# One transformer block on one core: ScalarE adds through PSUM in the last down-projection products, and the up projection's input sums are handed out 3, 3, 2, 2, 2, 0

## The chip, the cores and the metric

The kernel runs on one core of one Trainium2 chip. A core has a matrix engine (TensorE, PE in the profile; PEld is its weight load), a vector engine (VectorE, DVE), a scalar engine (ScalarE, ACT), a general engine (GpSimd, POOL) and a queue that starts transfers (SyncE, SP). Each engine works through its own list of instructions in order and waits on semaphores for the others. Matrix products land in PSUM, an accumulator memory of eight banks here; a tile `pall` of 128 x 4096 float32 covers all of them, 512 columns a bank. Everything else lies in SBUF or in the chip's main memory.

The metric is the device time of one execution, in microseconds (us).

## What is computed

One layer of a hybrid network for 1024 tokens of width 1024: a root-mean-square norm and an input projection, a sparse attention branch and a recurrent branch (RWKV7), gates, an output projection with a residual, and then a feed-forward part with a short convolution. The change touches only that last part (`w_up` goes from 1024 to 2 x 2816 columns, `w_down` from 2816 to 1024):

```python
def _conv_ffn(h, w_up, conv_w, w_down):
    u = h @ w_up
    u = lax.conv_general_dilated(u, conv_w[:, None, :], window_strides=(1,),
                                 padding=((CONV_WIDTH - 1, 0),),
                                 dimension_numbers=('NWC', 'WIO', 'NWC'),
                                 feature_group_count=u.shape[-1])
    a, b = jnp.split(u, 2, axis=-1)
    return (jax.nn.silu(a) * b) @ w_down
...
        x = x + _conv_ffn(_rms_norm(x, norm_ffn[l]), ffn_up[l], ffn_conv[l], ffn_down[l])
```

All values are float32. The kernel splits each operand into two float16 parts, high and low, and forms a product as three matrix products (high x high, high x low, low x high) that add up in one PSUM bank. Weights are scaled by `WS` = 256 before the split, so a finished bank holds 256 times the product and is multiplied by `WI` = 1/256 on its way out.

## The kernel before

Tokens are handled in two halves of 512 (h = 0 and h = 1), columns in blocks of 128. The program is written as one Python function that records instructions; a list scheduler with a simulated clock then decides the order of each engine's list. It takes the order of the program as a preference and keeps all data dependencies. `tc.issue_after(x)` adds one more rule: what is recorded inside comes behind `x` on `x`'s own engine.

**The up projection** has 22 pairs of column blocks (a for the SiLU, b for the product). For the first `NE` = 6 pairs the second half of the tokens is computed plainly, in the loop at line 1644: for each of six groups two series of 24 matmuls (`mm3`, called at line 1661, records them at L277), the convolution taps on ACT and DVE (`taps`, L1537 to L1542), and SiLU of the group before (`silu`, L1548 to L1550). The other 16 pairs (loop at line 1719) use a scheme with seven products of half size in place of eight (`prod`, L1675), which needs sums and differences of the inputs. These are T1 to T4, for four blocks k = 0 to 3. They are prepared by the generators `tprep(k)` (line 1559), each in three steps:

1. two subtractions on DVE (t3 and t1, L1569),
2. high parts of T3 and T1 on ACT (L1563), their low parts on DVE (L1564), and two further subtractions (t2 and t4),
3. high and low parts of T2 and T4 in the same way.

`TSTEPS` (line 68) says which generators take a step after each of the six plain groups; the steps come behind the group's last tap on ACT (`lasts[0]`). The first `prod` for pair 6 needs T1 and T2 of all four k. The low parts of the weights of the plain groups are made on DVE too (`split8`, L1609), and the weights run five groups ahead (`PFD`).

**The down projection** sums over 22 blocks of the hidden width, in the order `DSEQ` = "nnsnsnsn". An "n" (`plain`, line 1786) takes two blocks and, for each of 16 outputs (m = 0 to 7, h = 0 and 1), runs six matmuls into one bank (L1807) and adds the bank to the running sum `acc[m, h]` on DVE (L1809). An "s" (`combined`, line 1818) takes four blocks by the seven-product scheme: `product` (line 1871) runs 24 matmuls for four banks (L1878). Three of its seven products, o2, o3 and o4, belong to one quarter of the output alone and are added to `acc` on DVE (L1887, `key` is set); the other four (a, b, d, e) are added to side sums `sacc`. After the last "s" the side sums are folded into `acc` by `merge` (line 1923) on DVE (L1928, L1931, L1938, L1941) and POOL (L1934, L1935, L1942, L1943).

The small sums and merges wait in a list `todo`. `tick` (line 1756) takes one of them behind each DVE add. In the last "s" the order of the products is o1 (a), o2, o5 (e), o6 (b), o7 (d), o3, o4; `merge(2)`, twelve entries, is put into `todo` behind o7. Of these, j = 0 and j = 1 give POOL adds to `acc[4, 0]` and `acc[5, 0]` while o3 is recorded, ahead of o4, whose key is (4, 0). The last "n" (blocks 20 and 21) sends each finished `acc[m, h]` out (L1811).

Banks are taken from four tags of two banks each, so a bank returns after eight groups of six matmuls.

Of the kernel before, what the change touches and what calls it, by code (L numbers as in the profile page):

```python
# [11 lines left out]
AF = mybir.ActivationFunctionType  # L12
# [52 lines left out]
WK = (0, 200)  # L65
LV = 20
NEW = 4
TSTEPS = [(0, 0), (0, 1), (1, 1), (2, 2), (2, 3), (3, 3)]
PFD = 5
DSEQ = "nnsnsnsn"  # L70
GD = 6
# [9 lines left out]
WS = 256.0  # L81
WI = 1.0 / WS
# [84 lines left out]
def build(tc, D, dbg=None, upto=99):  # L167
    nc = tc.nc
    V, A, G, T = nc.vector, nc.scalar, nc.gpsimd, nc.tensor
    dbg = dbg or {}  # L170

    def load(t, src):
        return nc.sync.dma_start(t, src)

    with ExitStack() as ctx:
# [36 lines left out]
        def ps(tag):  # L212
            b = banks[tag]
            b.append(b.pop(0))
            return pall[:, 512 * b[-1]:512 * b[-1] + 512]
# [14 lines left out]
        H = [slice(0, 512), slice(512, 1024)]  # L230
# [1261 lines left out]
        with ExitStack() as st:  # L1492
# [18 lines left out]
            last = None  # L1511
            for k in range(8):
# [4 lines left out]
                last = V.tensor_sub(h2lo[1][k], hf, h2hi[1][k]).ins  # L1517
# [71 lines left out]
        def wraw(src, scale="A", behind=None):  # L1589
            rn_[0] += 1  # L1590
            x_ = rn_[0] // 2 % 2
            raw = (wp, fp)[x_].tile([128, 8, 128], F32, name="wraw", bufs=2)
            lastw[0] = load(raw, src).ins
            if scale == "A":
                with tc.issue_after(behind) if behind is not None else ExitStack():
                    A.activation(raw, raw, AF.Copy, scale=WS)
            elif scale == "G":
                G.tensor_scalar(raw, raw, WS, 0.0, op0=ALU.mult, op1=ALU.add)
            return raw
# [44 lines left out]
        for i in range(NE):  # L1644
            us = []
            if i == NE - 1:
                g_ = prep_up(NE)
                w = next(g_)
# [4 lines left out]
            for o in range(2):  # L1653
                n = 2 * i + o + PFD
# [4 lines left out]
                pj = pjs[o]  # L1659
# [7 lines left out]
            with tc.issue_after(lasts[0]):  # L1667
                for k in TSTEPS[i]:
                    next(tg[k])
# [12 lines left out]
        acc = {}  # L1682
# [36 lines left out]
        for i in range(NE, 22):  # L1719
# [26 lines left out]
            w = wn  # L1746
# [7 lines left out]
        todo = []  # L1754

        def tick(ins):
            if todo:
                with tc.issue_after(ins.ins):
                    todo.pop(0)()
# [6 lines left out]
        def pset(n):  # L1766
            r = []
            for _ in range(n):
                p = pring[0] % 12
                pring[0] += 1  # L1770
                tags = ["T%d%s%d" % ((2, 1, 4)[p // 4], c, p % 4) for c in "hl"]
                r.append([tf(t).tile([128, 512], F16, name="hh" + t[2], tag=t) for t in tags])
            return r

        def slot():
            n = wn_[0] % 4
            wn_[0] += 1
            if n % 2 == 0:
                return [wp.tile([128, 8, 128], F16, name=t, bufs=2) for t in ("whi", "wlo")]
            return [fp.tile([128, 8, 128], F16, name=t, bufs=2) for t in (("s12h", "s12l"), ("s34h", "s34l"))[n // 2]]  # L1780

        def cut(dst, src, e):
            A.activation(dst[0], src, AF.Copy)
            e.tensor_sub(dst[1], src, dst[0])  # L1784

        def plain(i0):
            hd_, wd_ = [], []
            for i in (i0, i0 + 1):
                raw = fp.tile([128, 2, 512], F32, name="thr", tag=("s12", "s34")[i % 2])
                hs = pset(2)  # L1790
                for h in range(2):
                    load(raw[:, h], th_d[h][i])
                    with tc.issue_after((seed, t_)[i0 // 2]) if i0 <= 2 else ExitStack():
                        cut(hs[h], raw[:, h], G)
                hd_.append(hs)
                w = slot()
                cut(w, wraw(D["f_dn"][i], behind=None if i0 else seed), V if i >= LV else G)
                wd_.append(w)
            yield
            for m in range(8):  # L1800
                for h in range(2):
                    pj = ps("PBAM"[(2 * m + h) % 4])
                    n = 0
                    for hs, (dh, dl) in zip(hd_, wd_):
                        hh, hl = hs[h]
                        for x, y in ((dh, hh), (dh, hl), (dl, hh)):
                            T.matmul(pj, x[:, m], y, start=(n == 0), stop=(n == 5))  # L1807
                            n += 1
                    tick(V.scalar_tensor_tensor(acc[m, h], pj, WI, acc[m, h], op0=ALU.mult, op1=ALU.add))  # L1809
                    if i0 == 20:  # L1810
                        nc.sync.dma_start(D["out"][m][:, H[h]], acc[m, h])  # L1811
# [6 lines left out]
        def combined(i0, first, last):  # L1818
# [52 lines left out]
            def product(ops_, n_, key, first=False):  # L1871
                w, hs = ops_
                for j in range(4):
                    pj = ps("PBAM"[j])
                    n = 0
                    for kp in range(2):
                        for x, y in ((0, 0), (0, 1), (1, 0)):
                            T.matmul(pj, w[x][:, 4 * kp + j], hs[kp][y], start=(n == 0), stop=(n == 5))  # L1878
                            n += 1
                    if key is None:  # L1880
                        d = sacc[n_, j]
                        if first:
                            A.activation(d, pj, AF.Copy, scale=WI)
                            continue
                    else:
                        d = acc[key[0] + j, key[1]]
                    tick(V.scalar_tensor_tensor(d, pj, WI, d, op0=ALU.mult, op1=ALU.add))  # L1887
# [12 lines left out]
            sums(2)  # L1900
            sums(3)
            product(o1, "a", None, first)
            o5 = sop(0, G)
            product(o2, None, (0, 0))
            flush()
            if last:
                merge(0)
            o6 = sop(1, V)
            product(o5, "e", None, first)
            o7 = sop(2, V)  # L1910
            product(o6, "b", None, first)
# [35 lines left out]
        seq, i0 = [], 0  # L1947
        for c in DSEQ:
            if c == "n":
                seq.append(plain(i0))  # L1950
                i0 += 2
            else:
                seq.append(combined(i0, "s" not in DSEQ[:len(seq)], "s" not in DSEQ[len(seq) + 1:]))
                i0 += 4
# [39 lines left out]
```

## Time and profile before

| | us |
|---|---|
| median of the runs | 1654.91 |
| the profiled execution | 1654.87 |
| its span, first to last instruction | 1653.1 |
| plain groups of the up projection, and the start of the seven-product part | about 1060 to 1148 |
| seven-product part of the up projection | about 1140 to 1430 |
| down projection | about 1430 to 1647 |
| its last "s" and last "n" | 1584.8 to 1647.3 |

The span is counted from the first to the last instruction; what lies around it is start and end of the program. Times in the text are microseconds from the start of the span. An engine is busy while an instruction of its own runs; a row of a group of instructions gives the line, the engine, the operation, what it writes and reads by the program's names, the shape, the count, the busy time in us, the mean duration in ns and the idle time in front of them with what ended it. In a timeline the brackets hold that idle time for one row. Successive instructions of one engine overlap a little, so the distance between starts is shorter than a duration: matmuls last 0.38 us and start every 0.216 us.

The middle of the down projection looks like this (columns: stretch, length, then the busy time of PE, PEld, DVE, ACT, POOL with instruction counts, the granted clock, DMA share, GB/s):

```profile
1507.00:1528.00 21.00, 21.00 (x99) 9.51 (x97) 18.89 (x26) 7.04 (x12) 9.55 (x7) 1.00 0.13 37
1528.00:1564.00 36.00, 36.00 (x168) 16.33 (x167) 29.92 (x40) 20.06 (x31) 27.72 (x21) 1.00 0.51 161
```

PE is busy there without a gap, in a plain pair (1507 to 1528) as in a combined block (1528 to 1564).

### The profile page before, as it was taken

How to read it: one execution, taken by the hardware profiler on the slowest of the kernel's cores; microseconds unless marked ns; L12 is line 12 of the kernel's file. 1: busy time of each engine (PE TensorE's matmuls, PEld its weight loads, DVE VectorE, ACT ScalarE, POOL GpSimd, SP SyncE). 2: the span in 40 equal slices, each digit the busy share in tenths (PEclk: the TensorE clock that was granted, in tenths of full speed). 3: DMA queues.
4: the chain of work that ended last, by engine and by line, in shares of the span. 5: the costliest groups of instructions: out<-in, count | busy, mean ns of one | idle time of the engine just before them, and what ended most of it. 6: DMA issues, size and time to landing. Idle time of an engine off the chain costs nothing. (4 is left out here: it accounts for less than half of the span.)

```text
span 1653.1 us, 30211 instructions
## 1 busy us (share of the span) xinstructions
PE 1617.4 (98%) x11856; PEld 851.6 (52%) x11856; DVE 1178.0 (71%) x1958; ACT 869.8 (53%) x1571; POOL 425.5 (26%) x344
## 2 busy tenths in 40 slices
PE   7999999999999999999999999999999999999997
PEld 3456555555555555666666444444444444444443
DVE  7545677778876548865558595598777777585898
ACT  5544675667657754556434453454554555645530
POOL 2101132021121220010001200214334333656756
PEclk9999999999999999999999999999999999999999
DMA  6352343232444456535555863453222223722402
GB/s 214 104 147 90 103 148 122 68 117 74 128 147 144 144 167 206 186 123 160 186 177 169 276 214 132 157 176 115 78 89 90 89 77 118 263 74 95 140 26 102
DMA packets 124687, 224.62 MB, mean 136 GB/s; under 512 B 16384, under 2 KB 45440, under 8 KB 124416
## 3 DMA queue, kind: packets, MB, share of 16 engines
q1 hardware_dynamic: 124544, 222.69, 40.6%
q8 instruction: 93, 1.52, 0.4%
q14 instruction: 50, 0.41, 0.1%
HBM read 153.86 MB, written 63.96 MB: 132 GB/s over the span
## 5 line engine op out<-in xcount | busy, mean ns | idle before, releaser
L277 PEld LDWEIGHTS <-whi 128*128 128x128 f16 x1808 | 173.1, 98 | 204.0 <-issue 9.0
L277 PE MATMUL pall<-hlo,whi 128*128 128x512 f16 x608 | 229.6, 379 | 2.1 <-DVE hlo L252 2.1
L277 PE MATMUL pall<-hhi,whi 128*128 128x512 f16 x608 | 229.2, 379 | 0.7 <-DVE zs L712 0.4
L277 PE MATMUL pall<-hhi,wlo 128*128 128x512 f16 x608 | 152.8, 379 | 0.0
L267 DVE SCALAR_TENSOR_TENSOR wlo<-wraw,whi 128x1024 f16<-128x1024 f32 (+1 forms) x98 | 109.7, 1119 | 56.6 <-PE pall L277 24.8
L265 ACT ACTIVATE whi<-wraw 128x1024 f16<-128x1024 f32 (+1 forms) x98 | 93.0, 950 | 107.7 <-PE pall L277 53.8
L672 DVE TENSOR_TENSOR pl<-pf,ph 128x512 f16<-128x512 f32 (+3 forms) x208 | 117.9, 577 | 38.9 <-ACT pf L671 38.0
L277 PEld LDWEIGHTS <-wlo 128*128 128x128 f16 x904 | 86.5, 98 | 98.0 <-issue 3.3
L670 ACT ACTIVATE ph<-pall 128x512 f16<-128x512 f32 (+3 forms) x208 | 99.8, 480 | 63.7 <-PE pall L665 33.2
L607 DVE TENSOR_REDUCE mp<-pall 128x1 f32<-128x512 f32 (+2 forms) x192 | 96.0, 516 | 36.1 <-PE pall L605 26.2
L671 ACT ACTIVATE pf<-pall 128x512 f32<-128x512 f32 (+3 forms) x208 | 100.5, 483 | 0.0
L1699 DVE SCALAR_TENSOR_TENSOR U<-pall,par,U 128x1023 f32<-128x1023 f32 x64 | 82.1, 1282 | 11.3 <-ACT U L1697 9.3
L1631 POOL TENSOR_TENSOR s<-wraw 128x512 f32<-128x512 f32 x16 | 28.0, 1748 | 191.2 <-DMA wraw<-f_up 183.6
L1402 POOL TENSOR_TENSOR b<-b,bonus 128x512 f32<-128x512 f32 x8 | 11.3, 1407 | 229.9 <-ACT b L1400 203.0
L694 POOL TENSOR_TENSOR onat<-onat,ot 128x256 f32<-128x256 f32 x32 | 29.5, 926 | 139.2 <-DVE ot L693 108.0
L675 PEld LDWEIGHTS <-ph 128*128 128x128 f16 x592 | 55.8, 96 | 16.1 <-ACT ph L670 3.0
L680 PEld LDWEIGHTS <-pl 128*128 128x128 f16 x592 | 55.6, 98 | 14.1 <-DVE pl L672 5.2
L1675 PEld LDWEIGHTS <-whi 128*128 128x128 f16 x384 | 37.6, 98 | 45.3
L1609 DVE SCALAR_TENSOR_TENSOR wlo<-wraw,whi 128x1024 f16<-128x1024 f32 (+1 forms) x35 | 47.6, 1360 | 17.2 <-PE pall L1675 12.9
L678 PEld LDWEIGHTS <-ph 128*128 128x128 f16 x592 | 55.9, 97 | 6.2 <-issue 1.3
L1809 DVE SCALAR_TENSOR_TENSOR acc<-pall,acc 128x512 f32<-128x512 f32 x80 | 51.7, 680 | 9.2 <-PE pall L1807 9.2
L1608 ACT ACTIVATE s12h<-s 128x1024 f16<-128x1024 f32 x16 | 16.9, 1056 | 67.3 <-POOL s L1632 66.0
(583 smaller groups left out, 4351.4 us busy)
## 6 DMA issues: line engine op xcount, KB each, us to landing
wraw<-f_up SPq DMA_DIRECT2D x56, 512.0 KB, 3.3
wraw<-w_t SPq DMA_DIRECT2D x46, 512.0 KB, 3.8
wraw<-f_dn SPq DMA_DIRECT2D x22, 512.0 KB, 3.4
sg_d<-zs SPq DMA_DIRECT2D x32, 256.0 KB, 2.4
wraw<-w_out SPq DMA_DIRECT2D x16, 512.0 KB, 3.8
th_d<-TH SPq DMA_DIRECT2D x32, 256.0 KB, 2.3
z_d<-zs SPq DMA_DIRECT2D x28, 256.0 KB, 2.8
x<-xT SPq DMA_DIRECT2D x24, 256.0 KB, 5.9
```

The lines of the kernel that those rows point to most:

```text
L265: A.activation(hi[:, :nk], raw, AF.Copy, scale=WS)
L267: V.scalar_tensor_tensor(lo[:, :nk], raw, WS, hi[:, :nk], op0=ALU.mult, op1=ALU.subtract)
L277: lastm[0] = T.matmul(ps, a[:, k], ks_(b, k), start=(n == 0), stop=(n == 3 * nk - 1)).ins
L607: V.reduce_max(mp[:, x, br, t:t + 1], pm[:, 0:(b1 - b0) * 128], axis=AX.X)
L670: A.activation(ph[0:nkey, rg], pa[0:nkey, rg], AF.Exp, scale=0.125)
L671: A.activation(pf[0:nkey, rg], pa[0:nkey, rg], AF.Exp, scale=0.125)
L672: V.tensor_sub(pl[0:nkey, rg], pf[0:nkey, rg], ph[0:nkey, rg])
L675: T.matmul(pov[:, t, :], ph[0:nkey, tk], vt[0:nkey, kb, g, 0:65], start=first, stop=False, skip_group_check=True)
L678: T.matmul(pov[:, t, 0:64], ph[0:nkey, tk], vt[0:nkey, kb, g, 65:129], start=False, stop=False, skip_group_check=True)
L680: T.matmul(pov[:, t, :], pl[0:nkey, tk], vt[0:nkey, kb, g, 0:65], start=False, stop=True, skip_group_check=True)
L1699: V.scalar_tensor_tensor(u[:, d:1024], c[:, 0:1024 - d], P("conv", 44 * (2 - d) + ci), u[:, d:1024], op0=ALU.mult, op1=ALU.add)
L1809: tick(V.scalar_tensor_tensor(acc[m, h], pj, WI, acc[m, h], op0=ALU.mult, op1=ALU.add))
```

## The change

Two edits.

The first sets `TSTEPS` anew: the twelve steps of the four generators are handed out 3, 3, 2, 2, 2, 0 to the six plain groups in place of 2 to each.

The second concerns additions to `acc`, in the last combined block (the three products with a `key`: o2, o3, o4, twelve banks) and in the last plain pair for h = 0 (eight banks). There ACT first writes 256 x `acc` into the bank (`seeded`), all six matmuls accumulate onto it (none starts the bank afresh), and ACT writes the bank times 1/256 back to `acc`. The DVE add is left out for these twenty banks. Entries of `todo` that hung on such an add are taken without an `issue_after` in `product`; in the last plain pair they are taken only at h = 1, so at every second bank.

```diff
-TSTEPS = [(0, 0), (0, 1), (1, 1), (2, 2), (2, 3), (3, 3)]
+TSTEPS = [(0, 0, 0), (1, 1, 1), (2, 2), (2, 3), (3, 3), ()]
...
+        def seeded(pj, src):
+            A.activation(pj, src, AF.Copy, scale=WS)
+
         def plain(i0):
...
                     n = 0
+                    sd = i0 == 20 and h == 0
+                    if sd:
+                        seeded(pj, acc[m, h])
                     for hs, (dh, dl) in zip(hd_, wd_):
                         hh, hl = hs[h]
                         for x, y in ((dh, hh), (dh, hl), (dl, hh)):
-                            T.matmul(pj, x[:, m], y, start=(n == 0), stop=(n == 5))
+                            T.matmul(pj, x[:, m], y, start=(n == 0 and not sd), stop=(n == 5), skip_group_check=sd)
                             n += 1
+                    if sd:
+                        A.activation(acc[m, h], pj, AF.Copy, scale=WI)
+                        nc.sync.dma_start(D["out"][m][:, H[h]], acc[m, h])
+                        continue
                     tick(V.scalar_tensor_tensor(acc[m, h], pj, WI, acc[m, h], op0=ALU.mult, op1=ALU.add))
...
                     pj = ps("PBAM"[j])
                     n = 0
+                    if key and last:
+                        seeded(pj, acc[key[0] + j, key[1]])
                     for kp in range(2):
                         for x, y in ((0, 0), (0, 1), (1, 0)):
-                            T.matmul(pj, w[x][:, 4 * kp + j], hs[kp][y], start=(n == 0), stop=(n == 5))
+                            T.matmul(pj, w[x][:, 4 * kp + j], hs[kp][y], start=(n == 0 and not (key and last)), stop=(n == 5),
+                                     skip_group_check=bool(key and last))
                             n += 1
+                    if key and last:
+                        A.activation(acc[key[0] + j, key[1]], pj, AF.Copy, scale=WI)
+                        if todo:
+                            todo.pop(0)()
+                        continue
                     if key is None:
```

## What I predicted, before the changed kernel had run

> **What bounds the kernel now.** I read the page's top first, then its chain, then a table of stretches around the two places that the diff touches, then each engine's timeline there.
>
> ```profile
> span 1653.1 us, 30211 instructions
> ...
> PE 1617.4 (98%) x11856; PEld 851.6 (52%) x11856; DVE 1178.0 (71%) x1958; ACT 869.8 (53%) x1571; POOL 425.5 (26%) x344
> ```
>
> TensorE (PE) is busy for 98% of the span, so a change that removes no matmul can win only PE's idle time, 1653.1 - 1617.4 = 35.7 us in the whole program, and what follows the last matmul. The stretches (columns: stretch, its length and the busy time of PE, PEld, DVE, ACT, POOL with counts, clock, DMA share, GB/s) say where some of it is.
>
> ```profile
> 1090.00:1110.00 20.00, 20.00 (x94) 9.10 (x93) 19.89 (x34) 12.29 (x19) 0.00 (x0) 1.00 0.54 183
> ...
> 1130.00:1150.00 20.00, 18.31 (x86) 8.23 (x85) 19.60 (x28) 7.96 (x13) 9.40 (x6) 1.00 0.45 158
> ...
> 1585.00:1600.00 15.00, 15.00 (x71) 6.82 (x70) 14.39 (x18) 8.13 (x13) 10.14 (x9) 1.00 0.10 35
> 1600.00:1610.00 10.00, 9.86 (x45) 4.21 (x44) 10.00 (x13) 3.77 (x6) 7.38 (x5) 1.00 0.16 52
> 1610.00:1620.00 10.00, 9.81 (x45) 4.39 (x45) 10.00 (x15) 1.06 (x1) 6.72 (x6) 1.00 0.01 2
> 1620.00:1630.00 10.00, 8.89 (x41) 3.80 (x39) 10.00 (x11) 0.00 (x0) 10.00 (x7) 1.00 0.00 0
> 1630.00:1640.00 10.00, 9.35 (x43) 3.89 (x41) 10.00 (x12) 0.00 (x0) 8.77 (x7) 1.00 0.21 80
> ```
>
> The reader is to see two things. At the end (from 1585) VectorE (DVE) has no free moment, PE loses time, and ScalarE (ACT) does almost nothing: 8.13 + 3.77 + 1.06 = 13.0 us in all. And between 1130 and 1150 PE loses 1.69 us in one piece. The PE timeline names both.
>
> ```profile
> 1147.96 0.38 PE L1675 MATMUL pall<-T1l,s12h 128*128 128x512 f16 x1 [1.69 <-DVE T1l L1564]
> ...
> 1584.80 0.38 PE L1878 MATMUL pall<-hhh,whi 128*128 128x512 f16 x1
> ...
> 1589.98 0.38 PE L1878 MATMUL pall<-hhh,s34h 128*128 128x512 f16 x1
> ...
> 1622.91 0.38 PE L1807 MATMUL pall<-hhh,s12h 128*128 128x512 f16 x1 [0.74 <-DVE acc L1887]
> ...
> 1645.78 0.38 PE L1807 MATMUL pall<-hhh,wlo 128*128 128x512 f16 x1
> ```
>
> Rows 1584.80 and 1589.98 are 24 matmuls apart (one product of four groups of six): 5.18 / 24 = 0.216 us a matmul. The end has seven such products (168 matmuls, L1878) and the last plain pair (96, L1807), 264 in all, so PE needs 264 x 0.2158 = 57.0 us. It took 1645.78 + 0.22 - 1584.80 = 61.2 us. So 4.2 us are gaps, each put down to a DVE operation that empties a bank late; TensorE has eight PSUM banks, one per group of six matmuls.
>
> **The first edit: input sums handed out 3, 3, 2, 2, 2, 0.** Nothing is added or removed. There are four generators of three steps. Before, group 5 (the last) still took the last two steps of k=3, and its T1l is the row that PE waits for at 1147.96. After, k=3 ends in group 4, one group of two matmul series earlier. That stall goes: -1.7 us. What is late next is nothing that I can find: the same timeline shows no other PE wait between 1150 and 1584, and whatever this stage feeds follows PE.
>
> What it costs: DVE does a part of this work earlier, in a stretch where it is busy 19.89 of 20.00 us. Step 1 is two subtractions, step 2 four, step 3 two.
>
> ```profile
> 1112.81 0.68 DVE L1564 TENSOR_TENSOR T1l<-t,T1h 128x512 f16<-128x512 f32 x1
> ...
> L1609 DVE SCALAR_TENSOR_TENSOR s34l<-wraw,s34h x4: 1207/1209/1217, 1077.7 to 1109.1; 128x1024 f16<-128x1024 f32 x4
> ...
> L277 PE MATMUL pall<-h2hi,s34l x32: 379/379/379, 1089.1 to 1137.3; 128*128 128x512 f16 x32
> ```
>
> After group 1 the hand-out is ahead by six subtractions of about 0.6 us, so DVE's other work is up to 3.6 us later. What PE waits for from that work is the low half of the next weights (L1609). The first s34l of that row is cut at 1077.7 and first multiplied at 1089.1, 11 us later; the last is cut at 1109.1, and its eight matmuls of 0.216 us end with the one at 1137.3, so they begin about 1135.8, 27 us later. 3.6 us fit into the smaller of the two. ACT's share (splits of T) runs where it is busy 12.29 of 20 us. I cost it at nothing; without that cover it would be at most 3.6 us. Value: -1.7, bounds -1.7 and +1.9.
>
> **The second edit: twenty adds leave DVE.** In the last combined block, the three products that go straight to `acc` (o2, o3, o4: 12 groups), and in the last plain pair the groups with h = 0 (8), lose their DVE multiply-add. Each gets two ACT passes: a seed of the bank with 256 x acc before the matmuls, and an eviction by 1/256 after them.
>
> ```profile
> 1640.09 7.25 DVE L1809 SCALAR_TENSOR_TENSOR acc<-pall,acc 128x512 f32<-128x512 f32 x12
> ...
> L1724 ACT ACTIVATE pall<-pall 128x512 f32<-128x512 f32 x16 | 9.4, 587 | 0.9 <-PE pall L1675 0.9
> ...
> L1739 ACT ACTIVATE u<-pall 128x512 f32<-128x512 f32 x16 | 9.3, 582 | 4.5 <-PE pall L1675 4.5
> ```
>
> Back to back the adds take 7.25 / 12 = 0.60 us each, so DVE loses 20 x 0.60 = 12.1 us. It is busy without a pause from 1586.3 to 1640.09 + 7.25 = 1647.34, 61 us; 49 us are left, less than the 57.0 us of PE. ACT's passes: no row shows a copy from SBUF into PSUM, so the seed is bounded by the two nearest forms, 0.58 (both ends in PSUM or out of it) and the 0.63 us of an SBUF copy below; I take 0.60 for each pass. 40 x 0.60 = 24 us on top of 13.0 is 37 of 61 us, so ACT has room. The Trainium skill says in "ScalarE: Activation LUTs", section "Rules for kernel authors", to put add and multiply on VectorE and not on ScalarE. This kernel's rows bear out half of it (1.2 us of ACT for 0.6 of DVE); it counts the engine's time, which here lies idle. By that rule alone the sum would carry 24 - 12 = +12 us, by the rows nothing.
>
> So the bank gaps, 4.2 us, can go. Bounds 0 and -4.2; I take -4.2, as 49 against 57 leaves DVE 8 us of room, and state separately what takes their place.
>
> **The new wait.** The old add read `acc` after the matmuls; the seed reads it before. Two seeds, of o4's groups 0 and 1, come behind adds of `merge` on POOL (L1934, then L1935), which the code hands out during o3. POOL waits there for DVE's partial sums.
>
> ```profile
> 1583.71 0.63 ACT L1783 ACTIVATE hhh<-thq 128x512 f16<-128x512 f32 x1 [5.36 <-PE pall L1807]
> ...
> 1614.66 1.27 POOL L1934 TENSOR_TENSOR sd<-sb,sd 128x512 f32<-128x512 f32 x1 [2.65 <-DVE sb L1931]
> ...
> 1621.13 2.25 POOL L1935 TENSOR_TENSOR acc<-acc,sd 128x512 f32<-128x512 f32 x1
> ...
> 1637.89 3.40 POOL L1943 TENSOR_TENSOR acc<-acc,sd 128x512 f32<-128x512 f32 x2
> ...
> L1935 POOL TENSOR_TENSOR acc<-acc,sd 128x512 f32<-128x512 f32 x4 | 6.9, 1735 | 1.2 <-DVE acc L1887 1.2
> ...
> L1934 POOL TENSOR_TENSOR sd<-sb,sd 128x512 f32<-128x512 f32 x4 | 6.0, 1490 | 3.3 <-DVE sb L1931 3.3
> ...
> L1887 DVE SCALAR_TENSOR_TENSOR acc<-pall,acc 128x512 f32<-128x512 f32 x12 | 7.9, 677 | 0.0
> ...
> L1931 DVE TENSOR_TENSOR sb<-sa,sb 128x512 f32<-128x512 f32 x4 | 4.6, 1141 | 0.0
> ```
>
> The order on POOL is sd0, sd1, acc of group 0, sd2, acc of group 1: the last ends at 1621.13 + 2.25 = 1623.4. DVE reaches the partial sums 4 x 0.60 = 2.4 us sooner (o2's adds are gone ahead of them), so I move that to 1621.0. A PE without gaps wants group 1 of o4 after 150 matmuls, at 1584.80 + 150 x 0.2158 = 1617.2, and its seed 0.7 us before. That is a wait of up to 4.5 us, if the written order stands. Against it: groups 2 and 3 of o4 need no add of POOL ahead of their seed and are 2 x 1.3 = 2.6 us of matmuls that the scheduler may place first. Behind the waiting seed on ACT stand o3's evictions and the next seeds, and PE waits for those too, but in the same stretch of time. I take the middle, +2.2, bounds 0 and +4.5. The other seeds read sums that are long done, or (rows 6 and 7) need POOL's adds by about 1636, and POOL's last of sixteen adds ended at 1641.3 with 3.3 + 1.2 us of waiting in it.
>
> A second page bears on POOL's speed: "SBUF — State Buffer" of the Trainium skill, section "SBUF: two separate sides", says that a DVE operation with two SBUF inputs and a POOL operation lock each other out. The last two rows fit that: 677 ns with one input in PSUM, 1141 ns for the add with both in SBUF while POOL works. The adds that leave DVE are of the first kind, so by that rule POOL gets no faster; without it five adds at the 1.27 of row 1614.66 would take 6.4 us and not the 8.7 to 1623.4, and the sum would be 2.2 us lower, with no wait left.
>
> **After the last matmul.** The results go out through SP, sixteen of 256 KB.
>
> ```profile
> 1646.00:1648.00 2.00, 0.16 (x1) 0.00 (x0) 1.34 (x3) 0.00 (x0) 0.00 (x0) 1.00 1.03 386
> 1648.00:1650.00 2.00, 0.00 (x0) 0.00 (x0) 0.00 (x0) 0.00 (x0) 0.00 (x0) 1.00 1.01 379
> ...
> DMA to landing us min/median/max: 2.0/3.3/4.2
> ```
>
> The twelve adds that DVE does at 0.60 us demand more than the 386 GB/s at which the DMA share stands at 1.0, so the last transfers queue. Paced by PE (one bank in 1.3 us, 202 GB/s) they would not. The last landing could then be 2.0 us after issue in place of 3.3: -1.3; the median row is the other end, 0. I take -1.0, since the pace lies at half the full rate.
>
> **Sum:** -1.7 - 4.2 + 2.2 - 1.0 = -4.7 us. The profiled execution took 1654.87 us (span 1653.1 and 1.8 around it), 0.04 under the median of the runs: 1654.87 - 4.7 = 1650.2 us. About 2% (33 us) is what a measurement of this kernel can tell from no change, and all the terms together are 7.2.
>
> **Rivals.**
> 1. No new wait, since the scheduler puts groups 2 and 3 of o4 first: 1654.87 - 1.7 - 4.2 - 1.0 = 1648.0. For it: 2.6 us of other matmuls, DVE with 8 us of room. Against it: POOL's order in the rows above.
> 2. The end is no shorter, because the seed wait eats the 4.2 us and the transfers still bunch; only the first edit pays: 1653.2. For it: 4.5 us by the written order.
> 3. Slower: POOL's add for group 1 of o4 ends no sooner than before, at 1623.4. Then the group starts at 1624.1, the 114 matmuls from there take 24.6 us, PE ends at 1648.7 and not 1646.0: +2.7 - 1.7 = 1655.9 with the transfers as they are. It decides from about 1622.4 on, where the loss equals the 1.7 of the first edit. For it: POOL waits for DVE's partial sums, whose order the scheduler may change. Against it: DVE is relieved before them.
> 4. ACT in the way: all twenty seeds are exposed, one behind another, 20 x 0.60 = 12 us: 1654.87 - 1.7 - 4.2 + 12 = 1661.0. Against it: 24 us of free ACT time and eight banks. This is what the ScalarE page's rule would make of it.
> 5. The first edit does not do what it says: another operation of DVE holds PE at 1146, or the crowded stretch takes it back. With the rest as forecast: 1651.9.
>
> **Chances.** Forecast 0.38, rival 1 0.25, rival 2 0.15, rival 3 0.10, rival 4 0.03, rival 5 0.09. The likeliest is 1650.2. Low end: every term at its best, 1654.87 - 1.7 - 4.2 - 1.3 = 1647.7, taken to 1647.2 for the rounding of rows. High end: between rivals 2 and 3, 1655.2, which leaves out rival 4 and most of rival 3. No case reaches 33 us either way: within 2% 0.985, faster 0.005, slower 0.01 for an order that the scheduler changes in a place that I do not see.
>
> **What would show it.** First edit: no row L1675 with a wait for T1l near 1147, and group 5 without T operations. Second: 20 fewer adds on L1809 and L1887, DVE with pauses after 1590, PE's waits for `acc` gone; in place of them a PE wait for an ACT write to `pall` near o4, or none (rival 1). End: less than 5.8 us (1653.1 - 1647.34) from the last add to the end of the span. Wrong would be a PE that still ends 61 us after the first matmul of the last combined block.

## The result, and the profile after

The changed kernel takes 1645.48 us (median of four runs, 1644.33 to 1646.61) against 1654.91 us for the kernel before on the same chip. That is the median of three runs; a fourth, at 1856.51 us, was a slow one and does not count. The ratio on record is 0.9946, with a 95% interval from 0.9934 to 0.9958 (the two medians alone give 0.9943). The forecast was 1650.2 us in a range from 1647.2 to 1655.2. The gain, 9.4 us, is twice the forecast's 4.7, and the time lies 1.7 us below the low end of the range. By the 2% bound the two kernels are the same, as forecast.

The top of the page, of the profiled execution of 1646.51 us:

```profile
span 1644.6 us, 30242 instructions
...
PE 1616.4 (98%) x11856; PEld 852.0 (52%) x11856; DVE 1164.0 (71%) x1938; ACT 891.4 (54%) x1611; POOL 424.2 (26%) x344
```

The counts are those of the diff: DVE has 20 instructions fewer, ACT 40 more, PE as many as before. The span is 8.5 us shorter. The stretches of the end, in the columns of the forecast's table (from 1584 to the end):

```profile
1584.00:1600.00 16.00, 16.00 (x75) 7.23 (x74) 15.27 (x20) 12.09 (x22) 12.08 (x8) 1.00 0.21 66
1600.00:1610.00 10.00, 10.00 (x48) 4.55 (x47) 9.29 (x14) 5.36 (x9) 6.58 (x6) 1.00 0.01 2
1610.00:1620.00 10.00, 10.00 (x48) 4.55 (x47) 10.00 (x8) 7.65 (x14) 10.00 (x7) 1.00 0.00 0
1620.00:1630.00 10.00, 10.00 (x48) 4.51 (x46) 7.75 (x8) 5.97 (x11) 10.00 (x7) 1.00 0.38 146
1630.00:1641.00 11.00, 10.97 (x51) 4.80 (x49) 3.88 (x5) 2.99 (x5) 3.60 (x3) 1.00 0.54 204
...
sum 60.60, PE 56.97 PEld 25.64 DVE 46.88 ACT 34.05 POOL 42.26; mean PE 9.49 PEld 4.27 DVE 7.81 ACT 5.68 POOL 7.04
```

Before, PE lost 0.14 to 1.11 us in each of these stretches from 1600 on; now it loses nothing. DVE is busy 46.88 us where 49 was estimated, ACT 34.05 us where 37 was. ACT's share, by groups of the same end (busy time, mean ns, idle time before), confirms the price of 0.60 us a pass that the kernel before had no row for:

```profile
L1787 ACT ACTIVATE pall<-acc 128x512 f32<-128x512 f32 x20 | 11.8, 597 | 7.9 <-DVE sd L1905 6.2 <-DVE acc L1819 1.2 <-DVE sb L1905 0.2
L1894 ACT ACTIVATE acc<-pall 128x512 f32<-128x512 f32 x12 | 6.8, 586 | 0.0
L1816 ACT ACTIVATE acc<-pall 128x512 f32<-128x512 f32 x8 | 4.8, 597 | 11.1 <-PE pall L1813 11.1
```

To cut the 8.5 us into pieces the reader needs a fixed point ahead of both edits. The first matmuls on L1508, which sum the squares for the feed-forward norm, are one. Their rows, first of the kernel before and then of the changed one (minimum, median and maximum ns, first and last start):

```profile
L1508 PE MATMUL pall<-sqs,ones x2: 592/592/592, 1048.5 to 1048.9; 128*128 128x512 f32 x2
```

```profile
L1508 PE MATMUL pall<-sqs,ones x2: 592/592/592, 1049.0 to 1049.4; 128*128 128x512 f32 x2
```

Everything ahead of this row is the same program, and yet it begins between 1047.8 and 1052.3 in the fourteen profiled executions of this study. That is run-to-run variation; "from the norm row" below means the span less the start of this row. Of three more rows of the changed kernel's PE timeline, the last two give the other cuts; the first is a small wait that the kernel before does not have, and e1 comes back to it:

```profile
1138.35 0.38 PE L1675 MATMUL pall<-h2h,whi 128*128 128x512 f16 x1 [0.21 <-DVE u L1542]
...
1583.82 0.38 PE L1890 MATMUL pall<-hhh,whi 128*128 128x512 f16 x1
...
1640.59 0.38 PE L1813 MATMUL pall<-hhh,wlo 128*128 128x512 f16 x1
```

| piece | before, us | after, us | difference | forecast |
|---|---|---|---|---|
| up to the norm row | 1048.5 | 1049.0 | +0.5 | 0 |
| norm row to the last combined block | 1584.8 - 1048.5 = 536.3 | 1583.8 - 1049.0 = 534.8 | -1.5 | -1.7 |
| its 264 last matmuls | 61.2 | 1640.59 + 0.22 - 1583.82 = 57.0 | -4.2 | -4.2 + 2.2 |
| behind the last matmul | 1653.1 - 1646.0 = 7.1 | 1644.6 - 1640.8 = 3.8 | -3.3 | -1.0 |

So two terms account for the miss: a new wait that did not come, and an end that shrank by 3.3 us in place of 1.0.

**Why no new wait came.** The seeds of o4's groups 0 and 1 do stand behind POOL's adds to `acc`. The two rows of the POOL timeline that answer to 1614.66 and 1621.13 of the kernel before:

```profile
1607.84 1.26 POOL L1952 TENSOR_TENSOR sd<-sb,sd 128x512 f32<-128x512 f32 x1 [0.63 <-DVE sb L1949]
...
1614.31 1.72 POOL L1953 TENSOR_TENSOR acc<-acc,sd 128x512 f32<-128x512 f32 x1
```

Counted from the first matmul of the block, POOL's add for group 1 now ends at 1614.31 + 1.72 - 1583.82 = 32.2 us, where it ended at 1623.38 - 1584.80 = 38.6 before. The forecast moved it by 2.4 us; it moved by 6.4. The DVE timeline says where the rest is from. Two of the products' input sums (the numbers in the names of `sq` shift by a few from kernel to kernel) in the kernel before, then in the changed one:

```profile
1596.02 1.04 DVE L1858 TENSOR_TENSOR sq__17159<-wraw,sq__17017 128x512 f32<-128x512 f32 x1
...
1602.86 0.68 DVE L1858 TENSOR_TENSOR sq__17177<-wraw,sq__17035 128x512 f32<-128x512 f32 x1
```

```profile
1575.49 0.68 DVE L1868 TENSOR_TENSOR sq__17161<-wraw,sq__17017 128x512 f32<-128x512 f32 x1
...
1581.02 0.68 DVE L1868 TENSOR_TENSOR sq__17181<-wraw,sq__17035 128x512 f32<-128x512 f32 x1
```

They have left the combined block for the plain pair ahead of it, and two sums of the same kind (`tq`, L1856) with them: about 3.5 us of DVE's work, done where DVE had room. DVE alone in four stretches, before and then after (columns: stretch, length, busy time and count, clock, DMA share, GB/s):

```profile
1575.00:1584.00 9.00, 7.36 (x12) 1.00 0.01 2
1584.00:1593.00 9.00, 7.79 (x10) 1.00 0.16 58
```

```profile
1575.00:1584.00 9.00, 9.00 (x13) 1.00 0.01 2
1584.00:1593.00 9.00, 8.97 (x12) 1.00 0.20 58
```

The program allows it because an entry of `todo` that is taken at o2, o3 or o4 no longer stands in an `issue_after` behind a DVE add. The scheduler may now put such an entry wherever its data allow, and at o2 the entries are input sums, whose data were there long before.

ACT, too, does not keep to the written order. The rows of its timeline that hold the seeds of o4:

```profile
1610.28 0.60 ACT L1787 ACTIVATE pall<-acc 128x512 f32<-128x512 f32 x1 [4.21 <-DVE sd L1905]
...
1613.86 0.60 ACT L1787 ACTIVATE pall<-acc 128x512 f32<-128x512 f32 x1 [2.00 <-DVE sd L1905]
...
1614.88 1.11 ACT L1787 ACTIVATE pall<-acc 128x512 f32<-128x512 f32 x2
...
1616.39 0.60 ACT L1787 ACTIVATE pall<-acc 128x512 f32<-128x512 f32 x1
```

The first two are groups 2 and 3, each right behind the DVE add (`sd`, the third and fourth of o7) that empties its bank. Group 0 is the first of the two seeds at 1614.88; the other belongs to the last pair. Group 1 is the one at 1616.39: it must stand behind POOL's add, which ended at 1616.03.

**Why the end shrank.** The SP queue of the kernel before: the last twelve issues as one row, then all sixteen by duration (minimum, median and maximum ns, first and last start). Behind it, the changed kernel's last issue and its times from issue to landing (2.0/3.3/4.2 before):

```profile
1640.79 8.51 SPq L1811 DMA_DIRECT2D out<-acc  x12
...
L1811 SPq DMA_DIRECT2D out<-acc x16: 332/390/1805, 1634.5 to 1648.8; - x16
```

```profile
1641.79 0.33 SPq L1821 DMA_DIRECT2D out<-acc  x1
...
DMA to landing us min/median/max: 2.0/2.0/4.3
```

Most of the 8.51 us is the pace of DVE's adds, one in 0.60 us, which the issues follow; an issue itself takes 0.39 us in the median, and one took 1.80. The last one came at 1648.8, 1.5 us after the last add ended (1647.34), and the last add ended 1.3 us after the last matmul. Now DVE's last add follows its matmul at once, and SP issues at once:

```profile
1641.07 0.69 DVE L1819 SCALAR_TENSOR_TENSOR acc<-pall,acc 128x512 f32<-128x512 f32 x1 [1.90 <-PE pall L1813]
```

The 3.3 us are thus three: the last add 0.4 us nearer to the last matmul (1641.76 - 1640.8 = 1.0 against 1.3), its transfer issued 1.4 us sooner behind it, and 1.5 us less from there to the end (1644.6 - 1641.8 = 2.8 against 4.3). They are stretches of one chain and not three causes: e12 takes most of the second away, and the third grows by nearly as much.

### The profile page after: what moved, and what is told of

It is laid out like the page before. It is cut to its first block, busy times and chain, and to the rows that moved or that the text cites. A ratio compares the mean times of both kernels' runs of the same rounds, so it can differ in the third digit from the quotient of the medians.

```text
span 1644.6 us, 30242 instructions
## 1 busy us (share of the span) xinstructions
PE 1616.4 (98%) x11856; PEld 852.0 (52%) x11856; DVE 1164.0 (71%) x1938; ACT 891.4 (54%) x1611; POOL 424.2 (26%) x344
## 4 chain that ended last, share of the span: by engine, by line
PE 60%; DVE 6%; ACT 2%; issue 1%; DMA 1%; POOL 0%; DVEq 0%; ACTq 0%
PE pall L277 18%; PE pall L1675 18%; PE pall L1890 7%; PE pall L1813 6%; PE pall L297 3%; PE pall L1227 1%; PE pall L1171 1%; DVE u L1540 1%; PE pall L1318 1%; DVE t L1569 1%; PE pall L1373 1%; PE pall L1378 1%; PE pall L1275 1%; PE pall L1268 1%; PE pall L1334 1%
## 5 line engine op out<-in xcount | busy, mean ns | idle before, releaser
L1675 PEld LDWEIGHTS <-whi 128*128 128x128 f16 x384 | 37.5, 98 | 45.8 <-issue 0.7
L1609 DVE SCALAR_TENSOR_TENSOR wlo<-wraw,whi 128x1024 f16<-128x1024 f32 (+1 forms) x35 | 48.5, 1385 | 17.9 <-PE pall L1675 12.5
L1819 DVE SCALAR_TENSOR_TENSOR acc<-pall,acc 128x512 f32<-128x512 f32 x72 | 47.1, 681 | 16.4 <-PE pall L1813 15.3
```

Of the source, the lines that this page charges most:

```text
L1675: T.matmul(bank, w[wi][:, o_ + k], xs_[k][xi], start=start and n == 0, stop=n == 11, skip_group_check=True)
```

## The experiments

The expectations give the theories letters, and not always the same. In e1 and e2, A says that the two edits are independent. In e4 and e8, A says that the adds must leave DVE; C, there and in e6, that the freed order does most of it, by letting DVE's sums go sooner. In e3, e10 and e11 it is A that stands for the freed sums; its rivals are B, the adds alone, and F, the freed merges at o3 and o4. In e5, A is both edits to the products together. D: the end is long where results bunch in the transfers; E: a landing takes a fixed 2.0 to 3.3 us and transfers run side by side; G: it is SP that issues too slowly. Kernels named e1 to e4, e5 to e8 and e9 to e12 each ran on one chip, with runs of the kernel before in between (medians 1656.16, 1656.17 and 1654.28 us); a ratio is against those. The columns in us are from one profile of each, cut as above: "gaps" is what the 264 last matmuls took over 57.0, "end" is what follows the last of them. In the six kernels without gaps these matmuls take 57.0 us, alike within 0.02. (Where an expectation gives the end of the change as 3.6 us, it is counted from the end of the last matmul's row, 1640.59 + 0.38.)

| kernel | from the norm row | gaps | end | median | ratio, 95% interval |
|---|---|---|---|---|---|
| before | 604.6 | 4.2 | 7.1 | | |
| the change | 595.6 | 0 | 3.8 | 1645.48 | 0.9946 (0.9934 to 0.9958) |
| e1, steps only | 602.9 | 4.3 | 6.4 | 1653.47 | 0.9988 (0.9976 to 0.9999) |
| e2, adds only | 596.6 | 0 | 3.8 | 1647.81 | 0.9959 (0.9944 to 0.9973) |
| e3, adds on ACT, all entries tied | 597.0 | 1.8 | 3.8 | 1648.63 | 0.9960 (0.9945 to 0.9975) |
| e4, adds on DVE, entries free | 597.8 | 0.9 | 5.2 | 1647.57 | 0.9954 (0.9939 to 0.9969) |
| e5, ACT in the products only | 595.2 | 0 | 3.9 | 1646.73 | 0.9945 (0.9922 to 0.9967) |
| e6, ACT in the last pair only | 599.4 | 4.1 | 4.0 | 1650.43 | 0.9969 (0.9949 to 0.9989) |
| e7, last results recorded together | 595.2 | 0 | 3.8 | 1645.56 | 0.9933 (0.9912 to 0.9954) |
| e8, e6 with entries free | 596.3 | 1.1 | 3.8 | 1646.94 | 0.9947 (0.9927 to 0.9966) |
| e9, last results held together | 600.6 | 0 | 9.3 | 1651.62 | 0.9979 (0.9965 to 0.9994) |
| e10, only the sums tied | 597.3 | 2.1 | 3.8 | 1649.54 | 0.9972 (0.9960 to 0.9983) |
| e11, only the merges tied | 595.3 | 0 | 3.9 | 1646.81 | 0.9954 (0.9934 to 0.9974) |
| e12, before, with two queues | 604.6 | 4.4 | 6.9 | 1653.73 | 0.9997 (0.9986 to 1.0009) |

### e1 and e2: one edit at a time

e1 is the kernel before with the new hand-out:

```diff
-TSTEPS = [(0, 0), (0, 1), (1, 1), (2, 2), (2, 3), (3, 3)]
+TSTEPS = [(0, 0, 0), (1, 1, 1), (2, 2), (2, 3), (3, 3), ()]
```

> Only the input sums are handed out 3, 3, 2, 2, 2, 0; the down projection is as before. Theory A (the two edits are independent; the changed kernel's stretch from the norm at 1049 to the last combined block is 1.35 us shorter): 1653.4 us, PE's wait for T1l gone, a wait of 0.2 us at the first L1675, and the end as before (4.2 us of gaps, 7.1 us from the last matmul to the end of the span). Rival: the earlier hand-out costs what it saves, 1654.5 to 1655.

e2 is the changed kernel with the old hand-out, the same two lines the other way round.

> Only the adds move to ACT; the input sums are handed out as before. Theory A: PE waits 1.7 us for T1l as before, then no gap in the last 264 matmuls (-4.2) and 3.6 us from the last matmul to the end in place of 7.1 (-3.5): 1647.2 us, ratio 0.9953. Rival (the edits help each other, the end is short only if PE comes early): 1649 or more.

The waits of PE in e1, and then in e2 (who waits on whom: total us, times, longest):

```profile
PE pall L1675 <- DVE u L1542: 0.4, 1, 0.4
```

```profile
PE pall L1675 <- DVE T1l L1564: 1.2, 1, 1.2
```

In e1 the wait for T1l is gone, and a smaller one, for the convolution's taps, has come in. It is not a stall that the old one had hidden: the matmul that waits is the first on L1675, 10 us ahead of the old stall. The last operation of these taps and this matmul in the kernel before, then the taps in the changed kernel (its matmul is the row at 1138.35 above):

```profile
1136.35 0.14 DVE L1542 TENSOR_TENSOR u<-u,edge 128x2 f32<-128x2 f32 x1
...
1137.47 0.38 PE L1675 MATMUL pall<-h2h,whi 128*128 128x512 f16 x1
```

```profile
1138.12 0.14 DVE L1542 TENSOR_TENSOR u<-u,edge 128x2 f32<-128x2 f32 x1
```

Counted from the norm row, the taps end at 1136.49 - 1048.5 = 88.0 us before and at 1138.26 - 1049.0 = 89.3 in the change, and PE is ready for them at 1137.47 - 1048.5 = 89.0. So DVE, with input sums handed to it earlier, reaches the taps 1.3 us later, and that uses up the 1.0 us that PE had to spare. (In e5 they are 0.6 us later, at 1138.27 - 1049.7 = 88.6, and PE does not wait.) A wait shows in e1, the change and e4 (0.2 to 0.4 us) and in none of the other eight kernels with the new steps.

From the norm row to the last combined block the kernels with the old steps take 536.3 (before), 535.8 (e2) and 536.3 us (e12). With the new ones it is 535.2 (e1), 534.8 (the change) and 534.7 us (e4) where the taps wait, and 534.4 us in each of the other eight. Against the mean of the first three, 536.1, the first edit brings 1.7 us without that wait and 0.9 to 1.4 with it. The gaps and the end belong to the second edit: e1 keeps its 4.3 us of gaps, e2 has none.

### e3 and e4: the passes or the order

e3 is the changed kernel with the entries at o2, o3 and o4 held again behind a DVE add, the last one before them:

```diff
         def tick(ins):
+            lv[0] = ins
...
                         if todo:
-                            todo.pop(0)()
+                            with tc.issue_after(lv[0].ins):
+                                todo.pop(0)()
                         continue
```

> The changed kernel, but the entries of todo taken in o2, o3 and o4 are held behind DVE's last add of the product before them, near to where the old tick put them. Theory A (untying let the scheduler draw four sums, 3.5 us of DVE, from o2 into the plain pair before, and that is why POOL's adds came 7.4 us sooner and not the 2.4 of the adds alone): the two L1868 rows come back behind 1590, the first merged sd starts about 3 us later, PE waits 0.5 to 2 us near o4: 1646 to 1647.5. Theory B (the adds alone are enough): the same rows move, but PE has no gap and the time is that of the changed kernel, 1645.5 within 0.6.

e4 leaves all twenty adds on DVE and only frees the entries:

```diff
                         d = acc[key[0] + j, key[1]]
+                    if key and last:
+                        V.scalar_tensor_tensor(d, pj, WI, d, op0=ALU.mult, op1=ALU.add)
+                        if todo:
+                            todo.pop(0)()
+                        continue
```

> The new hand-out of input sums, all adds on DVE as before, but the entries of todo taken in o2, o3 and o4 are not held behind DVE's adds. Theory C (the order alone is most of the gain): DVE has 3.5 us less to do behind 1585, 57.5 against PE's 57.0, gaps of at most 1.5 us, and 1649 to 1650.5. Theory A (it takes the adds off DVE): gaps of 3 to 4 us remain and the end still takes 6 to 7 us: 1652 to 1653.4.

| gaps / end, us | entries tied | entries free |
|---|---|---|
| adds on DVE | 4.3 / 6.4 (e1) | 0.9 / 5.2 (e4) |
| adds on ACT | 1.8 / 3.8 (e3) | 0 / 3.8 (the change) |

Freeing the entries, with not one add moved, takes out 3.4 us of gaps; moving the adds with the entries tied takes out 2.5. The passes and the order both have a part, and the parts overlap. (In e3 all entries of a product hang on one add ahead of it, a looser tie than in e1, so 2.5 is rather too much for the adds. Its median is above the 1647.5 us expected at most, e4's below the 1649 that theory C gave.) At the end the passes are worth more (2.6 us against 1.2), as DVE must have caught up with PE by the last bank. The timed ratios of e3 and e4 cannot be told apart, which agrees with 597.0 against 597.8 us. Nor do the intervals of e4 and of the change lie apart: that the passes add something to the freed order (595.6 against 597.8 us) rests on the profiles. What is left in e4 is of the old kind: the matmuls on L1807 wait twice, 0.4 us in all, for a bank that DVE's adds to `acc` (L1888) empty late.

### e5, e6 and e8: which of the passes

e5 moves only the twelve adds of the products:

```diff
-                    sd = i0 == 20 and h == 0
+                    sd = False
```

> The changed kernel, but the last plain pair adds on DVE as before; only o2, o3 and o4 go through ACT, untied. Theory A (the product's adds and their untying end the gaps, the plain pair's adds only shorten the end): no gap or one of under 0.5 us in the last 264 matmuls, 4 to 5.5 us after the last matmul, 58 + 4.5 = 61 to 62.5 us from the last combined block's first matmul to the end (60.6 in the changed kernel, 68.3 before). Rival (the plain pair carries it): gaps of 1 us or more.

e6 moves only the eight of the last pair; `product` is as before, entries tied:

```diff
-                    if key and last:
+                    if False:
                         seeded(pj, acc[key[0] + j, key[1]])
...
-                    if key and last:
+                    if False:
                         A.activation(acc[key[0] + j, key[1]], pj, AF.Copy, scale=WI)
```

> The changed kernel, but o2, o3 and o4 add on DVE and their entries of todo hang on these adds, as before; only the last plain pair goes through ACT for h = 0. Theory C (most of the gaps come from the tied order in the product): gaps of 2 to 3.5 us up to the first plain groups, then none; the end at 3.6 to 4.5 us, since half of the results no longer wait for DVE: 63 to 65 us from the block's first matmul to the end. Rival (eight adds less are enough): gaps under 1 us.

e8 is e6 with the entries freed as in e4.

> The changed kernel, but o2, o3 and o4 add on DVE, with their entries of todo not held behind these adds; the last plain pair goes through ACT for h = 0. Theory C (untying is what the product needs, ACT there is not): no gap or under 0.7 us, 3.6 to 4 us after the last matmul, 60.6 to 61.5 us from the block's first matmul to the end. Theory A (the twelve adds must leave DVE too): gaps of 0.9 us or more, as with all adds on DVE, 61.5 us or more.

The eight passes of the last pair bring nothing once the other twelve are there: e5 takes 595.2 us from the norm row, the change 595.6, and its end, 3.9 us, is below the 4 to 5.5 that was expected. Alone, in e6, they turn DVE's lateness into a wait of another name. The longest PE wait of e6's timeline, and the only one of e8's:

```profile
1623.40 0.38 PE L1813 MATMUL pall<-hhh,s12h 128*128 128x512 f16 x1 [1.39 <-ACT pall L1787]
```

```profile
1627.98 0.38 PE L1813 MATMUL pall<-hhh,s12h 128*128 128x512 f16 x1 [0.86 <-ACT pall L1787]
```

A seed cannot go into a bank before DVE has emptied it, nor before the sum that it carries is complete. Where DVE is late, the seed is, and the matmul waits for ACT in place of DVE. e6's 4.1 us of gaps are nearly those of e1 (4.3) and above the 2 to 3.5 that theory C gave; of the 3.5 us that it gains over e1, 2.4 lie in the end. e8's 1.1 us of gaps speak for theory A: with the entries free, the last microsecond of gaps goes only when the twelve adds of the products leave DVE too.

### e10 and e11: sums or merges

Both are e3 with a condition. e10 holds only the entries at o2, the sums; e11 holds those at o3 and o4, the merges (`!=` in place of `==`):

```diff
+                            with tc.issue_after(lv[0].ins) if key == (0, 0) else ExitStack():
+                                todo.pop(0)()
```

> The changed kernel, with only the four sums that are taken in o2 held behind DVE's last add before it; the merge entries in o3 and o4 stay free. Theory A (the sums, 3.5 us of DVE drawn into the plain pair before, are what untying brings): most of the 1.8 us of gaps with everything held come back, 1 to 2 us, by PE waits for an ACT seed. Rival F (the merge order is what matters): no gap.

> The changed kernel, with only the merge entries taken in o3 and o4 held behind DVE's last add before them; the sums in o2 stay free. Theory A: no gap or under 0.5 us. Rival F: 1 to 2 us of PE waits for an ACT seed.

e11 equals the change (595.3 and 595.6 us, no gap), e10 has all of e3's loss and a little more. F falls: it is the input sums at o2. The profile of e10, DVE, POOL, ACT and PE in turn, shows the chain that the forecast had looked for, with another holder:

```profile
1596.13 0.68 DVE L1871 TENSOR_TENSOR sq__17161<-wraw,sq__17017 128x512 f32<-128x512 f32 x1
...
1619.45 0.68 DVE L1909 SCALAR_TENSOR_TENSOR sd<-pall,sd 128x512 f32<-128x512 f32 x1
```

```profile
1620.16 0.60 ACT L1790 ACTIVATE pall<-acc 128x512 f32<-128x512 f32 x1 [2.00 <-DVE sd L1909]
...
1620.61 1.72 POOL L1957 TENSOR_TENSOR acc<-acc,sd 128x512 f32<-128x512 f32 x1
...
1620.81 0.38 PE L1893 MATMUL pall<-hhh,whi 128*128 128x512 f16 x1 [1.56 <-ACT pall L1790]
```

The sum is back at 1596, DVE empties the bank of o7's last group only at 1620.1, ACT seeds it then, and PE has waited 1.56 us; 0.20 more follow. POOL's add for group 1, at 1620.61, begins after that seed and cannot be what it waited for. From the first matmul of the block (1586.7 in e10) that add ends at 35.6 us, 3.0 sooner than before; the forecast had said 2.4.

### e7, e9 and e12: the end

e7 records the last eight results behind the loop, in reverse:

```diff
+            if i0 == 20:
+                for q in range(15, 7, -1):
+                    nc.sync.dma_start(D["out"][q // 2][:, H[q % 2]], acc[q // 2, q % 2])
```

> The changed kernel, but the last eight results are sent out together, behind the very last one. Theory D (at the end of the kernel before, transfers had queued at the full DMA rate, and this is what made 7.1 us of the 3.6): eight transfers of 262144 bytes at 386 GB/s are 5.4 us, so the end is 3.6 + 7 x 0.68 = 8.4 us long, and the issues on SP stretch beyond 0.33 us each. Rival E (the landing alone is a fixed 2.0 to 3.3 us and transfers run side by side): 5 to 6.5 us.

It tests nothing. The scheduler sent each result as it was ready all the same:

```profile
1634.86 9.23 SPq L1825 DMA_DIRECT2D out<-acc  x8
```

These are eight issues spread over 9.23 us, as PE's pace makes them, and the end is 3.8 us as without the edit. e9 forces what e7 wanted:

```diff
+            if i0 == 20:
+                f_ = nc.sync.dma_start(D["out"][7][:, H[1]], acc[7, 1])
+                with tc.issue_after(f_.ins):
+                    for q in range(8, 15):
+                        nc.sync.dma_start(D["out"][q // 2][:, H[q % 2]], acc[q // 2, q % 2])
```

> The changed kernel, with the last eight transfers held on SP's queue behind the very last result's (the try before let the scheduler send them as they came). Theory D (transfers that come together queue at the full DMA rate): eight times 262144 bytes at 386 GB/s are 5.4 us from the first issue, so the end is 3.6 + 7 x 0.68 = 8.4 us long. Rival E (a landing is a fixed 2.0 to 3.3 us and transfers run side by side): 3.6 + 7 x 0.33 us of issue = 5.9 us at most.

The last DVE add, the seven issues on SP behind it, and the stretches after the last matmul in e9:

```profile
1639.41 0.69 DVE L1820 SCALAR_TENSOR_TENSOR acc<-pall,acc 128x512 f32<-128x512 f32 x1 [1.90 <-PE pall L1813]
...
L1827 SPq DMA_DIRECT2D out<-acc x7: 332/433/647, 1640.6 to 1644.3; - x7
```

```profile
1642.00:1644.00 2.00, 0.00 (x0) 0.00 (x0) 0.00 (x0) 0.00 (x0) 0.00 (x0) 0.72 1.02 381
1644.00:1646.00 2.00, 0.00 (x0) 0.00 (x0) 0.00 (x0) 0.00 (x0) 0.00 (x0) 0.50 1.01 378
```

The last add is as prompt as in the change, and still the end is 9.3 us: E, with 5.9 at most, falls. D holds, though its 8.4 was 0.9 short. The DMA share stands at 1.0 at 378 to 381 GB/s, as it did at the end of the kernel before. e4 shows the same unforced: its last add ends at 1641.01 + 0.69 = 1641.7, 1.0 us behind the last matmul as in the change, and its end is 1.4 us longer, with a median landing of 3.3 us as in the kernel before, where the change has 2.0.

e12 is the kernel before with every second result sent from ACT's queue, which is idle there:

```diff
-                        nc.sync.dma_start(D["out"][m][:, H[h]], acc[m, h])
+                        (nc.sync, nc.scalar)[h].dma_start(D["out"][m][:, H[h]], acc[m, h])
```

> The kernel before, with the results of h = 1 sent from ACT's queue and those of h = 0 from SP's. Theory D (DMA engines at their full rate set the end): the gaps stay at 4.2 us and the end at 6 to 7.1 us. Rival G (SP's issue, which took 8.51 us for the last twelve where one alone takes 0.33, sets the end): the end falls to 4.5 to 5.5 us.

Its end is 6.9 us against 7.1, and the ratio has 1 in its interval. DVE's last adds, the issues of both queues and the landings:

```profile
1639.87 7.25 DVE L1809 SCALAR_TENSOR_TENSOR acc<-pall,acc 128x512 f32<-128x512 f32 x12
...
L1811 SPq DMA_DIRECT2D out<-acc x8: 332/333/909, 1634.3 to 1646.6; - x8
L1811 ACTq DMA_DIRECT2D out<-acc x8: 338/382/1492, 1636.0 to 1647.4; - x8
...
DMA to landing us min/median/max: 2.0/4.4/5.0
```

The last add ends at 1639.87 + 7.25 = 1647.1 and the last issue comes at 1647.4, 0.3 us later, where it came 1.5 us later with one queue. So the second queue does take SP's lag away, and the median landing grows from 3.3 to 4.4 us. G falls: the transfers hold the end, and not the issues.

## Why the forecast was wrong

**The step that failed for the time: "The new wait", +2.2.** It was priced with the entries of `todo` in their old places: "DVE reaches the partial sums 4 x 0.60 = 2.4 us sooner". The text before the forecast does note that entries in `product` are taken without an `issue_after`, and the forecast gave that no term. e10 measures it: with the sums tied again the gaps are 2.1 us, with them free nothing. That +2.2 is near the 1.8 and 2.1 us of the kernels with the order kept (e3, e10) is luck: PE's wait there is for a bank that DVE empties late and not for POOL's add. With the 3.5 us of DVE's sums moved ahead of the block, POOL's add ends 32.2 us behind the block's start, 0.5 us later than the forecast wanted the seed (1617.2 - 0.7 - 1584.8 = 31.7); the scheduler covered that by putting groups 2 and 3 first, as rival 1 had it. Whether either would have done alone was not tried. POOL itself got no faster, as the forecast had it: its sixteen adds took 25.1 us before (6.9 + 6.0 + 6.3 + 5.9) and 25.7 after (6.8 + 6.5 + 6.4 + 6.0).

**The step that failed for the range: "After the last matmul", -1.0 with bounds 0 and -1.3.** That transfers bunch was right (e9, e12). The size was not: the bounds counted one of three stretches, the time from issue to landing, and took it from the median row. The lag of the last add and the lag of the issue behind it, 1.3 and 1.5 us in the kernel before, can be read from that trace (the last matmul 1646.0, the last add 1647.34, the last issue 1648.8) and were left out. Measured, -3.3: two us beyond the bound. With every term at its best the forecast reached -7.2, so the time had to fall out of the range once the other terms came near their best.

**The first edit, -1.7.** Right in its mechanism, and in its size where the taps do not wait. The feared cost in the crowded stretch, set at nothing, is small but there: the forecast looked at the low halves of the weights (L1609), and what PE came to wait for is the taps (`u`, L1542), 0.2 to 0.4 us in three kernels of eleven.

**The bank gaps, -4.2.** Right as a sum: 264 matmuls in 57.0 us. The reason given, 12.1 us less for DVE, is part of it. e4 removes 3.4 of e1's 4.3 with DVE's 12.1 us in place, because what DVE lacked in this stretch was not only time but leave to work ahead in the stretch before, where it was busy 7.36 of 9.00 us.

**ACT has room.** Right: 34.05 of 60.6 us, each pass at 0.59 to 0.60. The section "Rules for kernel authors" of the page "ScalarE: Activation LUTs" of the Trainium skill, by which adds belong on DVE, would have added 12 us; the trace shows none of it while DVE is the late engine. e6 does show a case on its side: passes on ACT that wait for DVE gain no gap back.

**The rivals.** Rival 1 (no new wait) was right in its main claim, at 1648.0 for 1645.5, and missed the end like the forecast. Rivals 2 to 5 fall: PE has no gap, POOL is not late, no seed is exposed, and the first edit does what it says.

The cheapest version found is e5: it needs 16 ACT passes fewer than the change and takes 595.2 us from the norm row. Its ratio, that of e7 and that of the change overlap throughout, so none of them can be called faster.

## What to carry to other kernels

When a diff takes an instruction away, list what was ordered behind it as well as what it cost: here the removed order was worth 3.4 us of gaps alone and the removed time 2.5. Price the end of a kernel as a chain, last matmul to last add to last issue to last landing, with each lag from its own row; where transfers queue, a lag that is taken out of one stretch comes back in the next. And where work is handed to a busy engine earlier, look for everything that it now overtakes, and for who waits on that.

## What was not expected of the hardware

The issue of a 256 KB store on SP took 0.33 us where stores were spaced (the change) and 0.33 to 0.65 us where seven were ready at once (e9). One issue of the kernel before took far longer, and not at the full rate of the transfers: in most of its time the DMA share was 0.34.

```profile
1641.99 1.80 SPq L1811 DMA_DIRECT2D out<-acc  x1
...
1642.60:1643.80 1.20, 1.20 (x7) 0.53 (x6) 1.20 (x3) 0.00 (x0) 0.00 (x0) 1.00 0.34 123
```

e12 has such issues on both queues (0.91 and 1.49 us at most). What causes them stays open.

An ACT pass from SBUF into PSUM takes 597 ns for 128 x 512 float32, as long as the passes out of PSUM in the last pair (597), little longer than those in the products (586) and shorter than the 0.63 us of a copy within SBUF. It was an interpolation in the forecast.

The same program, up to the norm row, took between 1047.8 and 1052.3 us in fourteen executions at a granted clock of 0.998 to 1.000, so one profile's span alone does not show a change of 4 us. What causes it stays open.
